# A hybrid encoder layer: the scan's decay rows and time steps computed another way, and its first part put in a program block of its own

## The chip, the cores and the metric

The kernel runs on one core of one Trainium2 chip. The metric is the device time of one execution in microseconds (us). Three runs of the kernel before took 1328.16, 1330.67 and 1332.90 us, so the median is 1330.67 us. One more execution was profiled; all rows below are from it.

## The reference

One encoder layer over 512 tokens of width 1024, in fp32. What is computed, cut to its core:

```
h = rms_norm(x);  z, xBC, dt_f, dt_b, q, k, v, gates = split(h @ w_in)
xs, B, C = split(silu(conv5(xBC)))                # depthwise, over tokens
dt = softplus(dt_raw + bias);  a = -exp(a_log)    # 32 heads, two directions
A = cumsum(dt * a) inside chunks of 128 tokens    # forward and backward
y = sum_s (C_l . B_s) exp(A_l - A_s) dt_s x_s     # inside a chunk, s <= l (or >=)
  + exp(A_l) C_l . state                          # what the chunks before carry in
y = group_rms_norm((y_f + y_b + D * xs) * silu(z));  ssd = y @ w_br_ssd
attn = windowed GQA with rotary q/k and a sink, @ w_br_attn
x += (sigmoid(g1) * ssd + sigmoid(g2) * attn) @ w_out
x += cross_attention(rms_norm(x), rms_norm(mem));  x += swiglu_ffn(rms_norm(x))
out = rms_norm(x)
```

The change touches the lines from `dt` to the inside of `y` (the "scan").

## The kernel before

All activations are held transposed: 128 partitions of channels by 512 tokens, eight such slabs for the width of 1024. A projection is one weight granule of 128 by 1024 (512 KB) that SyncE (SP) loads (line 120, tile `raw`); ScalarE (ACT) rounds it to a high part `whi` (line 128), VectorE (DVE) or, for some, GpSimd (POOL) makes the low part `wlo` (line 129), and TensorE (PE) runs 24 matmuls of 512 columns into one PSUM bank `mm` (lines 138 to 140: high by high, high by low, low by high). `raw` has two buffers, `whi` and `wlo` three, and a load is written two granules ahead of its use.

The stages in order: keys and values of the memory, the norm of x, the scan branch in four groups of eight heads, attention, the merge, cross-attention, the FFN. The scan branch ends near 562 us of the span.

`dt_step` (line 338) comes once, ahead of the groups. It has the 64 rows of raw time steps (32 heads, two directions) as 64 partitions by 512 tokens in `x1`, and makes softplus there on DVE with a polynomial (lines 348 to 358: fourteen alternating multiplications and additions, lines 354 and 355, a reciprocal, line 349, and others). Three results are then turned to token rows by twelve PE transposes (line 368). From them come the cumulative decays: `fm` (line 380), written to DRAM as `adr` (line 383), and `nb`, `wt`, `dec`, which stay on the chip.

For each head, `head` (line 522) takes two rows of `adr`, each spread by DMA over all 128 partitions (tile `rt`, line 516, three buffers). ACT makes their exponentials for the later scaling into `ear` (line 528, one tile for a pair of heads, two buffers); POOL masks both triangles (line 530); for direction 0 ACT makes exp(row + nb) in four instructions of 128 columns (line 536), for direction 1 DVE adds `nb` in four (line 538) and ACT makes one exponential of 512 columns (line 539). `both` adds the two on POOL (line 545), `times` multiplies by `cb` on DVE (line 550, tile `mt`). `inner` (PE, line 560) uses `mt`, `arrive` (line 572) the carried states, `gather` (lines 580 to 585) scales the second by `ear` and adds, its last addition on POOL (line 585). `weigh` (POOL, line 492, tile `xw`) and `carry` (PE, line 500) build the states. `conv` (lines 408 to 414) is the convolution after a projection; `x_turn` (line 467) transposes a finished `xs` on PE, one or two projections later.

Work is written as a list of `steps`, scan steps woven between projections, and the framework turns the list into one instruction stream for each engine. An engine takes its stream strictly in order: an instruction that waits holds all behind it on its engine; SP's loads are such a stream too.

Of the kernel before, what the change touches and what calls it, by code (L numbers as in the profile page):

```python
# [37 lines left out]
V_DTB, V_AL, V_DSK, V_SNK = 200, 201, 202, 218  # L38
V_N = 234
# [23 lines left out]
RAWB, WB = 2, 3  # L63

# [8 lines left out]
def bidir_hybrid_layer(ctx: ExitStack, tc: tile.TileContext, io, dbg=None):  # L73
# [17 lines left out]
    adr = dram.tile([64, S], F32, tag="adr", name="adr")  # L91

# [245 lines left out]
    def dt_step(w):  # L338
        acc = proj(w, st["hh"], st["hl"])
        v, e, den, s2, pl = (x1[0:64, i] for i in range(5))  # L340

        def t256(i, o):
            return x1[:, i, 256 * o:256 * o + 256].rearrange("p (c e) -> p c e", c=NCH)

        nc.scalar.activation(v, acc[0:64], AF.Identity, bias=vec[0:64, V_DTB:V_DTB + 1])
        nc.scalar.activation(e, v, AF.Abs)
# [5 lines left out]
        nc.vector.tensor_scalar(pl, s2, 2.0 / 17.0, 2.0 / 15.0, op0=ALU.mult, op1=ALU.add)  # L352
        for n in (13, 11, 9, 7, 5, 3, 1):
            nc.vector.tensor_tensor(pl, pl, s2, op=ALU.mult)
            nc.vector.tensor_scalar(pl, pl, 2.0 / n, None, op0=ALU.add)
        nc.vector.tensor_tensor(pl, pl, e, op=ALU.mult)
        dt, dta, ld = den, s2, e
        nc.vector.scalar_tensor_tensor(dt, v, 0.0, pl, op0=ALU.max, op1=ALU.add)
        an = st["sp"].tile([64, 1], F32, tag="an", name="an")
        nc.scalar.activation(an, vec[0:64, V_AL:V_AL + 1], AF.Exp)  # L360
        nc.vector.tensor_scalar(dta, dt, an, -1.0, op0=ALU.mult, op1=ALU.mult)
        nc.vector.tensor_scalar(ld, dt, 1e-37, None, op0=ALU.max)
        nc.scalar.activation(ld, ld, AF.Ln)

        def tok(src, o):
            b = bank("sb")
            for c in range(NCH):
                nc.tensor.transpose(b[:, c * 64:(c + 1) * 64], src[:, c * P:(c + 1) * P], ident[0:64, 0:64])
            nc.scalar.copy(o, b[:, 0:256].rearrange("p (c e) -> p c e", c=NCH))
            return o  # L370

        dat = tok(dta, t256(5, 0))
        dtt = tok(dt, t256(5, 1))
        ldt = tok(ld, t256(7, 1))
# [3 lines left out]
        for d in range(2):  # L378
            for c in range(NCH):
                nc.tensor.matmul(fm[32 * d:32 * d + 32, c * P:(c + 1) * P], dat[:, c, 32 * d:32 * d + 32],  # L380
                                 tri[d], start=True, stop=True)
        nc.scalar.copy(x1[0:64, 6], fm[0:64])
        nc.sync.dma_start(adr, x1[0:64, 6])
        tm = bank("sb")
        tv = tm[:, 0:256].rearrange("p (c e) -> p c e", c=NCH)
        for d in range(2):
            nc.tensor.matmul(tv[:, :, 32 * d:32 * d + 32], tri[d], dat[:, :, 32 * d:32 * d + 32],
                             start=True, stop=True)
        tot = bank("sb")
        ov = tot[:, 0:256].rearrange("p (c e) -> p c e", c=NCH)  # L390
        nc.tensor.matmul(ov, ones, dat, start=True, stop=True)
        acm = t256(4, 0)
        nc.scalar.copy(acm, tv)
        nc.scalar.activation(dec, ov, AF.Exp)
        nc.vector.tensor_tensor(nb, ldt, acm, op=ALU.subtract)
        nc.vector.tensor_tensor(wt, ov, acm, op=ALU.subtract)
        nc.scalar.activation(wt, wt, AF.Exp)
        nc.vector.tensor_tensor(wt, wt, dtt, op=ALU.mult)
# [87 lines left out]
    def group_scan(g):  # L486
# [355 lines left out]
    win = io["w_in"]  # L842
    opens("mo")
# [320 lines left out]
def layout(inputs):  # L1164
# [22 lines left out]
    vecs[0:32, V_AL] = a["a_log_fwd"][0]  # L1187
    vecs[32:64, V_AL] = a["a_log_bwd"][0]
# [34 lines left out]
```

## Time and profile before

| what | value |
|---|---|
| median of three runs | 1330.67 us |
| the profiled execution | 1331.93 us |
| its span (first to last instruction) | 1330.2 us |
| PE busy | 1259.6 us, 95% of the span |
| DVE, ACT, POOL busy | 811.2, 579.1, 316.4 us |
| mean granted clock of PE | 0.984 of full speed |

"Busy" adds up the time in which an engine has an instruction at work. On PE matmuls overlap, so it says that PE has work, not that it runs at its best rate. The views below list, besides busy time, what ended each idle stretch of an engine ("waits"), and the clock that PE was granted, as a share of 2.4 GHz.

### The profile page before, as it was taken

Reading aid. Unit: us, or ns where it says so; the run is one execution under the profiler, and the core shown is the slowest. Engines: PE = TensorE matmul, PEld = TensorE weight load, DVE = VectorE, ACT = ScalarE, POOL = GpSimd, SP = SyncE. Lnnn points to the kernel's source line nnn. Section 1 sums busy time; section 2 is a strip of 40 time slices with the busy share of each in tenths; the row PEclk is TensorE's granted clock in tenths of the full one; section 3 lists DMA queues with packets and bytes.
Section 4 is the critical chain, followed back from the end, with each engine's and each line's share of the span. In section 5 each row is a group of like instructions: output and inputs, shape, how many; then the busy total and the mean of one; then the engine's idle time right before and its main releaser. Section 6 shows DMA issues by size and latency. Waiting matters only on the chain.

```text
span 1330.2 us, 16362 instructions
## 1 busy us (share of the span) xinstructions
PE 1259.6 (95%) x6084; PEld 1016.9 (76%) x6084; DVE 811.2 (61%) x1359; ACT 579.1 (44%) x1001; POOL 316.4 (24%) x259
## 2 busy tenths in 40 slices
PE   6879998998999899999999999999999999999996
PEld 5667777786777687887667888888888888888886
DVE  5896788789678876678875334665443334442323
ACT  6437366266346434167865223444332223332220
POOL 3344263244354452321000002001121111110001
PEclk9999999999999899999999999999999999999998
DMA  6425344243233332321103333411232332223331
GB/s 241 141 97 151 123 151 127 60 131 116 82 103 111 95 96 90 113 88 64 49 33 111 98 98 106 143 64 52 92 96 97 102 102 95 96 91 103 88 99 64
DMA packets 45440, 134.95 MB, mean 101 GB/s; under 512 B 5104, under 2 KB 8560, under 8 KB 45360
## 3 DMA queue, kind: packets, MB, share of 16 engines
q1 hardware_dynamic: 43072, 129.77, 30.8%
q10 hardware_dynamic: 1584, 2.03, 0.5%
q0 software_dynamic: 704, 2.10, 0.4%
q8 instruction: 48, 0.79, 0.2%
q14 instruction: 32, 0.26, 0.1%
HBM read 129.55 MB, written 4.33 MB: 101 GB/s over the span
## 4 chain that ended last, share of the span: by engine, by line
PE 62%; DVE 12%; issue 10%; POOL 7%; ACT 5%; DMA 2%; SPq 0%; DVEq 0%; POOLq 0%; ACTq 0%
PE mm L138 18%; PE mm L139 18%; PE mm L140 18%; DVE rt L538 2%; DVE cvu L411 2%; DVE wlo L129 2%; POOL vv L585 1%; PE sb L815 1%; POOL mt L545 1%; ACT whi L128 1%; PE sb L802 1%; DMA rt<-adr 1%; POOL rsw L714 1%; POOL rt L530 1%; PE sb L988 1%
## 5 line engine op out<-in xcount | busy, mean ns | idle before, releaser
L128 ACT CAST whi<-raw 128x1024 fp32r<-128x1024 f32 (+2 forms) x192 | 198.9, 1037 | 451.9 <-PE mm L139 388.2
L138 PE MATMUL mm<-hh,whi 128*128 128x512 f32 x968 | 384.9, 398 | 6.9 <-DVE cvu L411 5.4
L139 PE MATMUL mm<-hl,whi 128*128 128x512 f32 x968 | 380.4, 393 | 1.8 <-DVE hl L310 1.8
L140 PE MATMUL mm<-hh,wlo 128*128 128x512 f32 x968 | 380.6, 393 | 1.1 <-DVE wlo L129 1.0
L129 DVE TENSOR_TENSOR wlo<-raw,whi 128x1024 fp32r<-128x1024 f32 (+2 forms) x193 | 242.4, 1257 | 128.4 <-ACT whi L128 122.4
L138 PEld LDWEIGHTS mm<-hh,whi 128*128 128x128 f32 x968 | 183.8, 190 | 46.3 <-issue 8.2
L140 PEld LDWEIGHTS mm<-hh,wlo 128*128 128x128 f32 x968 | 183.4, 189 | 41.3 <-DVE wlo L129 2.9
L139 PEld LDWEIGHTS mm<-hl,whi 128*128 128x128 f32 x968 | 183.6, 190 | 39.3 <-DVE hl L310 3.0
L185 POOL TENSOR_TENSOR sq_acc<-sq_acc,sq 128x512 f32<-128x512 f32 x14 | 24.8, 1771 | 264.4 <-ACT sq L184 264.4
L1041 POOL TENSOR_TENSOR fa<-fa,row 128x512 f32<-128x512 f32 x22 | 39.1, 1776 | 192.4 <-ACT fa L1040 192.4
L411 DVE SCALAR_TENSOR_TENSOR cvu<-mm,hcw,cvu 128x510 f32<-128x510 f32 (+1 forms) x96 | 70.9, 739 | 4.3 <-ACT cvu L408 3.9
L138 PE MATMUL mm<-vh,whi 128*128 128x512 f32 (+1 forms) x192 | 72.5, 378 | 0.0
L138 PE MATMUL mm<-fh,whi 128*128 128x512 f32 (+1 forms) x198 | 72.4, 366 | 0.0
L139 PE MATMUL mm<-fl,whi 128*128 128x512 f32 (+1 forms) x198 | 72.4, 365 | 0.0
L140 PE MATMUL mm<-fh,wlo 128*128 128x512 f32 (+1 forms) x198 | 72.4, 365 | 0.0
L140 PE MATMUL mm<-vh,wlo 128*128 128x512 f32 (+1 forms) x192 | 70.0, 364 | 0.0
L139 PE MATMUL mm<-vl,whi 128*128 128x512 f32 (+1 forms) x192 | 69.5, 362 | 0.0
L538 DVE TENSOR_SCALAR rt<-rt,nb 128x128 f32<-128x128 f32 x128 | 52.4, 465 | 21.3 <-POOL rt L530 19.6
L545 POOL TENSOR_TENSOR mt<-rt 128x512 f32<-128x512 f32 x32 | 47.7, 1493 | 72.1 <-ACT rt L539 34.1
L1043 DVE TENSOR_TENSOR ft<-fa,mm 128x512 f32<-128x512 f32 x22 | 15.1, 688 | 73.2 <-PE mm L140 71.0
L528 ACT ACTIVATE ear<-rt 64x1024 f32<-64x1024 f32 x32 | 33.9, 1059 | 56.6 <-POOL vv L585 51.9
L139 PE MATMUL mm<-ol,whi 128*128 128x512 f32 x128 | 50.0, 391 | 0.0
(234 smaller groups left out, 2061.4 us busy)
## 6 DMA issues: line engine op xcount, KB each, us to landing
raw<-in_w_in SPq DMA_DIRECT2D x69, 512.0 KB, 3.5
raw<-in_w_fi SPq DMA_DIRECT2D x44, 512.0 KB, 3.5
rt<-adr SPq DMA_DIRECT2D x64, 256.0 KB, 4.4
raw<-in_w_bs SPq DMA_DIRECT2D x16, 512.0 KB, 3.4
raw<-in_w_fo SPq DMA_DIRECT2D x16, 512.0 KB, 3.5
raw<-in_w_xk SPq DMA_DIRECT2D x8, 512.0 KB, 3.8
raw<-in_w_ba SPq DMA_DIRECT2D x8, 512.0 KB, 3.5
raw<-in_w_mo SPq DMA_DIRECT2D x8, 512.0 KB, 3.5
```

The lines of the kernel that those rows point to most:

```text
L128: nc.scalar.copy(hi[:, t], raw[:, t])
L129: (nc.gpsimd if i in LO_POOL else nc.vector).tensor_tensor(lo[:, t], raw[:, t], hi[:, t].bitcast(F32), op=ALU.subtract)
L138: nc.tensor.matmul(acc, wh, xh[:, k0 + k], start=first and k == 0, stop=False)
L139: nc.tensor.matmul(acc, wh, xl[:, k0 + k], start=False, stop=False)
L140: nc.tensor.matmul(acc, wl, xh[:, k0 + k], start=False, stop=last and k == nk - 1)
L185: eng.tensor_tensor(acc, acc, sq, op=ALU.add)
L411: nc.vector.scalar_tensor_tensor(u[:, b], acc[:, a], w5[j], u[:, b], op0=ALU.mult, op1=ALU.add)
L528: nc.scalar.activation(st["ear", h // 2][own], rt[own], AF.Exp)
L538: nc.vector.tensor_scalar(r, r, st["nb"][:, c, e0:e0 + 1], None, op0=ALU.add)
L545: nc.gpsimd.tensor_tensor(mt, st["rt", g, h][:, 0], st["rt", g, h][:, 1], op=ALU.add)
L1041: nc.gpsimd.tensor_tensor(a, a, st["row2"], op=ALU.mult)
L1043: nc.vector.tensor_tensor(t, a, st["fp", 2 * j + 1], op=ALU.mult)
```

## The change

Five things are done, all ahead of the end of the scan branch.

1. `dt_step` turns the raw time steps to token rows first (four transposes, line 352 of the new kernel) and does softplus on 128 partitions by 256, with each multiplication and addition of the polynomial in one instruction (line 364). `a_log` arrives as a row for every partition, so `vecs` is 297 columns wide, not 234.
2. The exponentials of the decay rows are made once, on 64 partitions (`erows`), and written to DRAM as `edr`; `ear` is filled from there by DMA, two loads a pair of heads (`earows`), in place of ACT's line 528.
3. Both directions of `rt` come in one DMA of 512 KB, not two of 256 KB.
4. For direction 1, ACT adds `nb` inside its exponential, in four instructions as for direction 0; DVE's line 538 and ACT's line 539 are gone.
5. The first part of the program, to the end of the scan branch, is a block in which the streams are ordered event by event along a timeline (`schedule_with_timeline_sim=True`); the rest is ordered as before. Each engine gets a branch into the block and one out of it. Behind the block the streams of PE, ACT, POOL and SP are the same as before, instruction for instruction (buffer numbers apart); DVE's differ at its first four places.

```diff
+EL = (2, 4)
...
     def dt_step(w):
         acc = proj(w, st["hh"], st["hl"])
-        v, e, den, s2, pl = (x1[0:64, i] for i in range(5))
-
-        def t256(i, o):
-            return x1[:, i, 256 * o:256 * o + 256].rearrange("p (c e) -> p c e", c=NCH)
-
-        nc.scalar.activation(v, acc[0:64], AF.Identity, bias=vec[0:64, V_DTB:V_DTB + 1])
-        nc.scalar.activation(e, v, AF.Abs)
+
+        def slot(i):
+            return x1[:, i // 2, 256 * (i % 2):256 * (i % 2) + 256].rearrange("p (c e) -> p c e", c=NCH)
+
+        v, e, den, s2, pl, dta, ld, acm = (slot(i) for i in range(8))
+        raw, rows, erows = (x1[0:64, i] for i in (5, 6, 7))
+        nc.scalar.activation(raw, acc[0:64], AF.Identity, bias=vec[0:64, V_DTB:V_DTB + 1])
+        tp = bank("sb")
+        tpv = tp[:, 0:256].rearrange("p (c e) -> p c e", c=NCH)
+        for c in range(NCH):
+            nc.tensor.transpose(tpv[:, c], raw[:, c * P:(c + 1) * P], ident[0:64, 0:64])
+        an = st["sp"].tile([P, 64], F32, tag="an", name="an")
+        nc.scalar.activation(an, vec[:, V_AL:V_AL + 64], AF.Exp)
+        nc.scalar.activation(e, tpv, AF.Abs)
+        nc.vector.tensor_copy(v, tpv)
         nc.scalar.activation(e, e, AF.Exp, scale=-1.0)
         nc.vector.tensor_scalar(den, e, 2.0, None, op0=ALU.add)
         nc.vector.reciprocal(den, den)
         nc.vector.tensor_tensor(e, e, den, op=ALU.mult)
         nc.vector.tensor_tensor(s2, e, e, op=ALU.mult)
-        nc.vector.tensor_scalar(pl, s2, 2.0 / 17.0, 2.0 / 15.0, op0=ALU.mult, op1=ALU.add)
-        for n in (13, 11, 9, 7, 5, 3, 1):
-            nc.vector.tensor_tensor(pl, pl, s2, op=ALU.mult)
-            nc.vector.tensor_scalar(pl, pl, 2.0 / n, None, op0=ALU.add)
-        nc.vector.tensor_tensor(pl, pl, e, op=ALU.mult)
-        dt, dta, ld = den, s2, e
+        nc.vector.tensor_scalar(pl, s2, 2.0 / 17.0, None, op0=ALU.mult)
+        for n in (15, 13, 11, 9, 7, 5, 3):
+            nc.vector.scalar_tensor_tensor(pl, pl, 2.0 / n, s2, op0=ALU.add, op1=ALU.mult)
+        nc.vector.scalar_tensor_tensor(pl, pl, 2.0, e, op0=ALU.add, op1=ALU.mult)
+        dt = den
         nc.vector.scalar_tensor_tensor(dt, v, 0.0, pl, op0=ALU.max, op1=ALU.add)
-        an = st["sp"].tile([64, 1], F32, tag="an", name="an")
-        nc.scalar.activation(an, vec[0:64, V_AL:V_AL + 1], AF.Exp)
-        nc.vector.tensor_scalar(dta, dt, an, -1.0, op0=ALU.mult, op1=ALU.mult)
+        anb = an.rearrange("p (o e) -> p o e", o=1).broadcast_to([P, NCH, 64])
+        nc.vector.scalar_tensor_tensor(dta, dt, -1.0, anb, op0=ALU.mult, op1=ALU.mult)
         nc.vector.tensor_scalar(ld, dt, 1e-37, None, op0=ALU.max)
-        nc.scalar.activation(ld, ld, AF.Ln)
-
-        def tok(src, o):
-            b = bank("sb")
-            for c in range(NCH):
-                nc.tensor.transpose(b[:, c * 64:(c + 1) * 64], src[:, c * P:(c + 1) * P], ident[0:64, 0:64])
-            nc.scalar.copy(o, b[:, 0:256].rearrange("p (c e) -> p c e", c=NCH))
-            return o
-
-        dat = tok(dta, t256(5, 0))
-        dtt = tok(dt, t256(5, 1))
-        ldt = tok(ld, t256(7, 1))
         nb, wt, dec = (st[n] for n in ("nb", "wt", "dec"))
         tri = [st["tri"][:, d] for d in range(2)]
...
-                nc.tensor.matmul(fm[32 * d:32 * d + 32, c * P:(c + 1) * P], dat[:, c, 32 * d:32 * d + 32],
+                nc.tensor.matmul(fm[32 * d:32 * d + 32, c * P:(c + 1) * P], dta[:, c, 32 * d:32 * d + 32],
                                  tri[d], start=True, stop=True)
...
+        nc.vector.tensor_copy(rows, fm[0:64])
+        nc.sync.dma_start(adr, rows)
+        nc.scalar.activation(erows, rows, AF.Exp)
+        nc.sync.dma_start(edr, erows)
         nc.scalar.copy(acm, tv)
         nc.scalar.activation(dec, ov, AF.Exp)
-        nc.vector.tensor_tensor(nb, ldt, acm, op=ALU.subtract)
         nc.vector.tensor_tensor(wt, ov, acm, op=ALU.subtract)
         nc.scalar.activation(wt, wt, AF.Exp)
-        nc.vector.tensor_tensor(wt, wt, dtt, op=ALU.mult)
+        nc.vector.tensor_tensor(wt, wt, dt, op=ALU.mult)
+        nc.scalar.activation(ld, ld, AF.Ln)
+        nc.vector.tensor_tensor(nb, ld, acm, op=ALU.subtract)
...
         def rows(h):
             rt = st["sp"].tile([P, 2, S], F32, tag="rt", name="rt", bufs=RB)
             e0 = 8 * g + h
-            for d in range(2):
-                nc.sync.dma_start(rt[:, d], adr[32 * d + e0:32 * d + e0 + 1, :].broadcast_to([P, S]))
+            nc.sync.dma_start(rt, adr.rearrange("(d e) s -> e d s", d=2)[e0:e0 + 1].broadcast_to([P, 2, S]))
             st["rt", g, h] = rt
+
+
+        def earows(i):
+            def f():
+                st["ear", i] = ear = st["sp"].tile([P, 2, S], F32, tag="ear", name="ear", bufs=2)
+                for k in range(2):
+                    e0 = 8 * g + 2 * i + k
+                    nc.sync.dma_start(ear[64 * k:64 * k + 64], edr.rearrange("(d e) s -> e d s", d=2)[e0:e0 + 1]
+                                      .broadcast_to([64, 2, S]))
+            return f
 
         def head(h):
             def f():
-                sp = st["sp"]
                 for n in (range(RB) if h == 0 else [h + RB - 1] if h + RB - 1 < HPG else []):
                     rows(n)
                 rt = st["rt", g, h]
-                if h % 2 == 0:
-                    st["ear", h // 2] = sp.tile([P, 2, S], F32, tag="ear", name="ear", bufs=2)
-                own = slice(64 * (h % 2), 64 * (h % 2) + 64)
-                nc.scalar.activation(st["ear", h // 2][own], rt[own], AF.Exp)
                 for d in range(2):
                     nc.gpsimd.affine_select(
                         out=rt[:, d].rearrange("p (c l) -> p c l", c=NCH),
                         in_=rt[:, d].rearrange("p (c l) -> p c l", c=NCH), pattern=[[0, NCH], [1 - 2 * d, P]],
                         base=0, channel_multiplier=2 * d - 1, compare_op=ALU.is_ge, fill=neg)
-                for c in range(NCH):
-                    r, e0 = rt[:, 0, c * P:(c + 1) * P], 8 * g + h
-                    nc.scalar.activation(r, r, AF.Exp, bias=st["nb"][:, c, e0:e0 + 1])
-                    r, e0 = rt[:, 1, c * P:(c + 1) * P], e0 + 32
-                    nc.vector.tensor_scalar(r, r, st["nb"][:, c, e0:e0 + 1], None, op0=ALU.add)
-                nc.scalar.activation(rt[:, 1], rt[:, 1], AF.Exp)
+                for d in range(2):
+                    for c in range(NCH):
+                        r, e0 = rt[:, d, c * P:(c + 1) * P], 32 * d + 8 * g + h
+                        nc.scalar.activation(r, r, AF.Exp, bias=st["nb"][:, c, e0:e0 + 1])
             return f
...
-                order.append(ga[(t - LAG3 - GLAG) // 2])
+                i = (t - LAG3 - GLAG) // 2
+                order += [ga[i]] + el[i + 2:i + 3]
+            if t in EL:
+                order.append(el[EL.index(t)])
...
+    cutat = len(steps)
     opens("mo")
     opens("at")
     add(at_open)
...
     ready, taken = [], 0
+    blk = ExitStack()
+    blk.enter_context(tc.block(schedule_with_timeline_sim=True))
     for i, (fn, gr) in enumerate(steps):
+        if i == cutat:
+            blk.close()
         ahead = LOOK if i >= lead else (i - lead + 4) // 2
         while len(ready) < min(len(specs), taken + len(gr) + ahead):
```

Three places show what is moved. The first is DVE at the end of the first group's scan, before: the four instructions of line 411 and line 414 finish a convolution into `xs`, which PE then transposes.

```order
L550 TENSOR_TENSOR mt_2004<-mt_2004,cb_1302 128x512
L411 SCALAR_TENSOR_TENSOR cvu_1770<-mm_1745,hcw_410,cvu_1770 128x510
L538 TENSOR_SCALAR rt_1989<-rt_1989,nb_170 128x128
L411 SCALAR_TENSOR_TENSOR cvu_1770<-mm_1745,hcw_410,cvu_1770 128x511
L129 TENSOR_TENSOR wlo_1794<-raw_1791,whi_1793 128x1024
L411 SCALAR_TENSOR_TENSOR cvu_1770<-mm_1745,hcw_410,cvu_1770 128x511
L538 TENSOR_SCALAR rt_1989<-rt_1989,nb_170 128x128
L411 SCALAR_TENSOR_TENSOR cvu_1770<-mm_1745,hcw_410,cvu_1770 128x510
L538 TENSOR_SCALAR rt_1989<-rt_1989,nb_170 128x128 x2
L550 TENSOR_TENSOR mt_2056<-mt_2056,cb_1302 128x512
L129 TENSOR_TENSOR wlo_1828<-raw_1825,whi_1827 128x1024
L414 SCALAR_TENSOR_TENSOR xs_1744<-cvt_1776,cvu_1770 128x512
```

The same place now, where the convolution has lines 409 and 412:

```order
L131 TENSOR_TENSOR wlo_1763<-raw_1760,whi_1762 128x1024
L409 SCALAR_TENSOR_TENSOR cvu_1739<-mm_1714,hcw_412,cvu_1739 128x510
L409 SCALAR_TENSOR_TENSOR cvu_1739<-mm_1714,hcw_412,cvu_1739 128x511 x2
L409 SCALAR_TENSOR_TENSOR cvu_1739<-mm_1714,hcw_412,cvu_1739 128x510
L131 TENSOR_TENSOR wlo_1797<-raw_1794,whi_1796 128x1024
L479 SCALAR_TENSOR_TENSOR zs_1791<-zs_1791,mm_1766 128x512
L412 SCALAR_TENSOR_TENSOR xs_1713<-cvt_1745,cvu_1739 128x512
L131 TENSOR_TENSOR wlo_1841<-raw_1838,whi_1840 128x1024
```

Four additions to `rt`, the multiplications into `mt` and one `wlo` no longer stand between the parts of the convolution.

The second is PE there. Before, the transpose of this `xs` stands between two projections (`mm_1831`, `mm_1876`):

```order
L139 MATMUL mm_1831<-hl_169,whi_1740 128x512
L140 MATMUL mm_1831<-hh_168,wlo_1741 128x512
L467 MATMUL sb_1859<-cst_77,xs_1744 128x128 x4
L138 MATMUL mm_1876<-hh_168,whi_1793 128x512
L139 MATMUL mm_1876<-hl_169,whi_1793 128x512
```

Now it stands inside the second of them, behind eleven of its 24 matmuls, the last three of which are shown:

```order
L142 MATMUL mm_1845<-hh_170,wlo_1763 128x512
L140 MATMUL mm_1845<-hh_170,whi_1762 128x512
L141 MATMUL mm_1845<-hl_171,whi_1762 128x512
L465 MATMUL sb_1828<-cst_78,xs_1713 128x128 x4
L142 MATMUL mm_1845<-hh_170,wlo_1763 128x512
L140 MATMUL mm_1845<-hh_170,whi_1762 128x512
```

The transpose has moved eleven matmuls back in PE's stream.

The third is SP at the start of the first group's scan. Before, where `adr` is written and the first rows are fetched:

```order
L120 DMA raw_848<-in_w_in 128x1024
L120 DMA raw_895<-in_w_in 128x1024
L383 DMA adr_74<-x1_69 64x512
L120 DMA raw_929<-in_w_xk 128x1024
L516 DMA rt_1084<-adr_74 128x512 x2
L516 DMA rt_1087<-adr_74 128x512 x2
L516 DMA rt_1090<-adr_74 128x512 x2
L120 DMA raw_975<-in_w_in 128x1024
```

Now:

```order
L122 DMA raw_833<-in_w_in 128x1024
L387 DMA adr_74<-x1_69 64x512
L389 DMA edr_75<-x1_69 64x512
L513 DMA rt_1069<-adr_74 128x2x512
L513 DMA rt_1071<-adr_74 128x2x512
L513 DMA rt_1073<-adr_74 128x2x512
L522 DMA ear_1162<-edr_75 64x2x512 x2
L522 DMA ear_1278<-edr_75 64x2x512 x2
L122 DMA raw_880<-in_w_in 128x1024
L122 DMA raw_914<-in_w_xk 128x1024
```

The write of `adr` stands one weight load earlier, `edr` and four loads of `ear` are new, and both weights that follow (`raw_880`, `raw_914`) stand behind all of them.

## Rows read from the trace of the kernel before

**Rows 1.** the page: span, busy time of each engine with its share

```profile
span 1330.2 us, 16362 instructions
...
PE 1259.6 (95%) x6084; PEld 1016.9 (76%) x6084; DVE 811.2 (61%) x1359; ACT 579.1 (44%) x1001; POOL 316.4 (24%) x259
```

**Rows 2.** busy time by stretch, us: PE, PEld, DVE, ACT, POOL; clock, DMA share

```profile
300.00:340.00 40.00, 33.38 (x158) 26.89 (x158) 33.43 (x54) 24.35 (x44) 15.52 (x15) 0.91 0.42 128
...
1000.00:1100.00 100.00, 100.00 (x443) 82.80 (x442) 41.82 (x48) 30.01 (x38) 16.05 (x9) 1.00 0.29 95
```

**Rows 3.** the waits of PE up to 562 us: total us, times, longest

```profile
PE sb L467 <- DVE xs L414: 19.9, 6, 5.7
...
PE mm L138 <- DVE cvu L411: 5.4, 3, 2.2
PE sb L500 <- POOL xw L492: 5.0, 6, 1.7
PE sb L368 <- DVE x L361: 4.2, 1, 4.2
PE sa L560 <- DVE mt L550: 2.9, 1, 2.9
```

**Rows 4.** PE in order of time, three of those: start, us, [idle before <- releaser]

```profile
193.80 0.65 PE L467 MATMUL sb<-cst,xs 128*128 128x128 f32 x4 [2.76 <-DVE xs L414]
...
225.06 0.63 PE L467 MATMUL sb<-cst,xs 128*128 128x128 f32 x4 [4.16 <-DVE xs L414]
...
333.11 1.09 PE L467 MATMUL sb<-cst,xs 128*128 128x128 f32 x4 [5.70 <-DVE xs L414]
```

**Rows 5.** busy time by stretch, the 20 us before one of those waits ends

```profile
205.00:225.00 20.00, 15.90 (x72) 12.80 (x71) 20.00 (x34) 13.87 (x26) 8.76 (x8) 1.00 0.52 157
```

**Rows 6.** the same with line 538 alone; the sum is over six stretches

```profile
205.00:225.00 20.00, 5.73 (x12) 1.00 0.52 157
...
sum 120.00, DVE 25.23; mean DVE 4.20
```

**Rows 7.** busy time in the eight half-clock stretches of the first 562 us

```profile
195.00:198.40 3.40, 3.40 (x23) 3.07 (x19) 1.70 (x2) 1.47 (x2) 2.24 (x2) 0.51 0.33 98
...
331.60:338.40 6.80, 5.29 (x15) 4.35 (x16) 4.99 (x7) 4.35 (x7) 2.11 (x2) 0.50 0.64 193
444.20:451.00 6.80, 5.92 (x20) 5.26 (x21) 5.42 (x9) 2.48 (x4) 3.06 (x3) 0.50 0.65 187
...
sum 34.00, PE 31.61 PEld 26.06 DVE 25.65 ACT 14.06 POOL 13.26; mean PE 3.95 PEld 3.26 DVE 3.21 ACT 1.76 POOL 1.66
```

**Rows 8.** groups by line, 0 to 566 us: busy us, mean ns, idle before

```profile
L538 DVE TENSOR_SCALAR rt<-rt,nb 128x128 f32<-128x128 f32 x128 | 52.4, 465 | 21.3 <-POOL rt L530 19.6 <-DMA raw<-in_w_in 1.7
...
L536 ACT ACTIVATE rt<-rt,nb 128x128 f32<-128x128 f32 x128 | 41.0, 391 | 0.5 <-POOL rt L530 0.2
...
L528 ACT ACTIVATE ear<-rt 64x1024 f32<-64x1024 f32 x32 | 33.9, 1059 | 56.6 <-POOL vv L585 51.9 <-DMA rt<-adr 4.2
...
L539 ACT ACTIVATE rt<-rt 128x512 f32<-128x512 f32 x32 | 19.9, 627 | 12.8 <-DVE rt L538 12.8
...
L398 DVE TENSOR_TENSOR wt<-wt,x 128x256 f32<-128x256 f32 x1 | 0.4, 420 | 0.0
```

**Rows 9.** time-step instructions on DVE: ns min/median/max, first and last start us

```profile
L354 DVE TENSOR_TENSOR x<-x x7: 670/672/2876, 67.7 to 86.2; 64x512 f32<-64x512 f32 x7
...
L349 DVE RECIPROCAL x<-x x1: 3333/3333/3333, 58.7 to 58.7; 64x512 f32<-64x512 f32 x1
```

**Rows 10.** the same by stretch: us, DVE busy (instructions), clock, DMA share

```profile
57.00:96.00 39.00, 26.82 (x23) 1.00 0.34 113
```

**Rows 11.** the waits of all engines, 0 to 566 us: total us, times, longest

```profile
ACT ear L528 <- POOL vv L585: 51.9, 14, 8.2
...
PEld mm L138 <- issue: 9.2, 16, 2.6
```

**Rows 12.** what the DMA queue on SP waited for, 0 to 566 us

```profile
SPq L120 <- DVE wlo L129: 305.7, 67, 15.5
```

More of the change, by code (lines that the diff above doesn't have):

```diff
@@ L37 @@
 V_CW, V_CB, V_SSD = 40, 160, 184
-V_DTB, V_AL, V_DSK, V_SNK = 200, 201, 202, 218
-V_N = 234
+V_DTB, V_DSK, V_SNK, V_AL = 200, 201, 217, 233
+V_N = 297
 G_DT, G_K, G_V, G_Q, G_GA, G_SSD, G_GS, G_N = 0, 1, 3, 5, 13, 21, 61, 69
@@ L91, in bidir_hybrid_layer @@
     adr = dram.tile([64, S], F32, tag="adr", name="adr")
+    edr = dram.tile([64, S], F32, tag="edr", name="edr")
     def bank(tag):
@@ L379, in dt_step @@
             for c in range(NCH):
-                nc.tensor.matmul(fm[32 * d:32 * d + 32, c * P:(c + 1) * P], dat[:, c, 32 * d:32 * d + 32],
+                nc.tensor.matmul(fm[32 * d:32 * d + 32, c * P:(c + 1) * P], dta[:, c, 32 * d:32 * d + 32],
                                  tri[d], start=True, stop=True)
-        nc.scalar.copy(x1[0:64, 6], fm[0:64])
-        nc.sync.dma_start(adr, x1[0:64, 6])
         tm = bank("sb")
@@ L386, in dt_step @@
         for d in range(2):
-            nc.tensor.matmul(tv[:, :, 32 * d:32 * d + 32], tri[d], dat[:, :, 32 * d:32 * d + 32],
+            nc.tensor.matmul(tv[:, :, 32 * d:32 * d + 32], tri[d], dta[:, :, 32 * d:32 * d + 32],
                              start=True, stop=True)
@@ L390, in dt_step @@
         ov = tot[:, 0:256].rearrange("p (c e) -> p c e", c=NCH)
-        nc.tensor.matmul(ov, ones, dat, start=True, stop=True)
-        acm = t256(4, 0)
+        nc.tensor.matmul(ov, ones, dta, start=True, stop=True)
+        nc.vector.tensor_copy(rows, fm[0:64])
+        nc.sync.dma_start(adr, rows)
+        nc.scalar.activation(erows, rows, AF.Exp)
+        nc.sync.dma_start(edr, erows)
         nc.scalar.copy(acm, tv)
         nc.scalar.activation(dec, ov, AF.Exp)
-        nc.vector.tensor_tensor(nb, ldt, acm, op=ALU.subtract)
         nc.vector.tensor_tensor(wt, ov, acm, op=ALU.subtract)
         nc.scalar.activation(wt, wt, AF.Exp)
-        nc.vector.tensor_tensor(wt, wt, dtt, op=ALU.mult)
+        nc.vector.tensor_tensor(wt, wt, dt, op=ALU.mult)
+        nc.scalar.activation(ld, ld, AF.Ln)
+        nc.vector.tensor_tensor(nb, ld, acm, op=ALU.subtract)
         dump("dt", dt)
@@ L605, in group_scan @@
         hd, bo, ti = ([w(h) for h in range(HPG)] for w in (head, both, times))
-        nn, ar, ga, gs = ([w(i) for i in range(4)] for w in (inner, arrive, gather, gate))
+        nn, ar, ga, gs, el = ([w(i) for i in range(4)] for w in (inner, arrive, gather, gate, earows))
         order = []
@@ L1186, in layout @@
     vecs[32:64, V_DTB] = a["dt_bias_bwd"][0]
-    vecs[0:32, V_AL] = a["a_log_fwd"][0]
-    vecs[32:64, V_AL] = a["a_log_bwd"][0]
+    vecs[:, V_AL:V_AL + 32] = a["a_log_fwd"][0][None]
+    vecs[:, V_AL + 32:V_AL + 64] = a["a_log_bwd"][0][None]
     vecs[:, V_DSK:V_DSK + 16] = _cols(np.repeat(a["d_skip"][0], 64))
```

## The prediction, made before the result was known

> **What bounds the kernel now.** The page is read first. PE is busy for 95% of the span, the next engine, DVE, for 61% [rows 1]. So PE sets the time, and the question is what PE loses. Second come the busy times by stretch. In the FFN, from 1000 to 1100 us, PE runs 443 matmuls of 512 columns in 100 us without a gap: 0.226 us each, its best rate, and DVE needs 42 of the 100 us. In the scan branch, from 300 to 340 us, PE is busy for 33.4 of 40 us at a mean clock of 0.91, and DVE for 33.4 as well [rows 2]. What can be won lies ahead of 562 us. Third come PE's own waits there. The largest kind by far is the transpose of a finished convolution (line 467) that waits for DVE's `xs`: 19.9 us in six places. Then come projections that wait for DVE to read a bank out (5.4), carries that wait for POOL's `xw` (5.0), the transposes in `dt_step` (4.2) and `inner` (2.9) [rows 3]. The order in time shows that the six are not noise: PE stands still for 2.8, 4.2 and 5.7 us with nothing else it may do [rows 4]. In the 20 us that end with the wait at 225 us DVE is busy for all 20 [rows 5], so PE waits there for a DVE that is behind. Fourth, the clock. Eight stretches ahead of 562 us, 34.0 us together, ran at 1.2 instead of 2.4 GHz [rows 7]. One begins at 195 us, right after the wait that ended at 193.8; one at 331.6, inside the wait that ends at 333.1. In them PE was busy for 31.6 us. Work at half rate costs half its time, so about 15.8 us were lost.
>
> **The change part by part.**
>
> Term A, the six transposes. Line 538 goes from DVE: 128 instructions, 52.4 us [rows 8]. In the six stretches of 20 us that end with the six waits it takes 25.2 us, more than the 19.9 us that PE waits; ahead of 225 us it is 5.7 us against a wait of 4.2 [rows 4, 6]. The order shows besides that the transpose at the end of the first group stands eleven matmuls later, worth 11 x 0.226 = 2.5 us, and that no `rt` work stands inside that convolution any more. Bounds: 0 (DVE fills the room with other work that is in front) and 19.9. I take 18, since relief exceeds the wait in sum and DVE, at 33.4 of 40 us in such a stretch, gives up 52.4 us over some 440 us of scan, near 5 in 40.
>
> ACT takes it over. For each head it had 1059 (ear) + 4 x 391 + 627 = 3250 ns; it will have 8 x 391 = 3128 ns [rows 8]. That is 0.1 us less a head, so nothing on ACT gets later. In such a stretch it is busy for 24.4 of 40 us [rows 2]. Cost: none. One load of `rt` in place of two carries the same bytes, and `vecs` is 32 KB larger: 0 for both, beside weight loads of 512 KB that PE does not wait for now.
>
> Term B, `dt_step`. On DVE its 23 instructions take 26.8 us between 57 and 96 us [rows 10], the reciprocal 3.3 of them [rows 9]. The new chain has twelve two-input instructions, a copy and three with a scalar on 128 x 256, each like the 0.42 us of line 398, and a reciprocal on half as many elements (half of 3.3): 16 x 0.42 + 1.7 = 8.4 us [rows 8, 9]. What hangs on DVE there is 4.2 us at the transposes and 5.4 us at the banks [rows 3]. Twelve transposes become four, which I don't count. Bounds 2 and 9.6; I take 7, nearer the upper end, for the chain is a third of what it was.
>
> Line 354 has a median of 672 ns, but one of its seven took 2876 [rows 9]; POOL makes `wlo` in that stretch. The Trainium skill (GPSIMD Engine Reference, Key points) says that GpSimd shares its SBUF interfaces with VectorE and contends with DVE instructions that have two SBUF inputs. That speaks against the new chain, whose steps nearly all have two: by the rule a few of them would take 2.2 us more, as that one did; with three such the chain is 15 us, term B 5 and not 7, and the sum 30 and not 32. The trace agrees as far as line 354 goes.
>
> Term C, the carries. Five us of waiting for POOL's `xw` come at the start of the groups, where POOL is late with masks because ACT's `ear` held it up: ACT stood 51.9 us waiting for POOL to free an `ear` [rows 11]. That hold is gone from ACT. POOL's own work stays. Bounds 0 and 5.0; I take 3.
>
> Term D, the clock. Of the eight half-clock stretches five follow waits of terms A and B (96, 195, 225.8, 331.6 and 444.2 us). Each of the three short ones costs 3.4/2 = 1.7, the two long ones 5.29/2 and 5.92/2 by their busy time [rows 7]: 3 x 1.7 + 2.6 + 3.0 = 10.7. Bounds 0 and 15.8; I take 9, since A and B are not taken in full either.
>
> Term E, what is new. First, in-order waits: the event order puts `inner` one instruction at a time between matmuls, where a late `mt` holds PE at once. The nearest row is the single wait of 2.9 us at `inner` [rows 3]; sixteen pairs of heads could each meet one, so the bounds are 0 and 46. I take 4, nearest to the row as it is. Second, SP: `ear` adds 32 loads of 256 KB, and ahead of the first group two weights stand behind seven loads. SP waits 305.7 us in 67 places for `wlo` to free a buffer [rows 12], 4.6 us a load, which is the slack that hides this; if it were gone, one load's wait would reach PE. I take 0 here, and the rival below prices it. Third, the border of the blocks. No row shows it: bounds 0 and 2.6, the longest that PE's weight loads stood for no reason shown [rows 11]; I take 1. The Trainium skill (Advanced Engine Details and Errata, Control Flow Timing) gives about 51 ns for a branch; by that the term would be 0.05 us, which no row here shows. Fourth, the start: all four loads of x now stand ahead of the third weight, which delays that weight and brings the norm forward; I take 0.
>
> Behind the block nothing moves on PE, so the 768 us from 562 to the end of the span stay.
>
> Sum: 18 + 7 + 3 + 9 - 4 - 1 = 32 us less. From the profiled execution's own 1331.9 us that gives 1299.9. The median of the runs is 1.3 us below the profiled one, so the forecast for a median is 1299 us.
>
> **The rivals.**
>
> *All waits go.* If the terms come at their upper bounds and the 2.9 us at `inner` go as well: 19.9 + 9.6 + 5.0 + 2.9 + 15.8 - 1 = 52 us, so 1279 us for a median. For it: with line 538 gone DVE has 12 of 40 us free, and in the FFN, where it has more, PE loses nothing [rows 2]. Against: one of the half-clock stretches (at 21 us) lies ahead of all that the change touches.
>
> *Half.* The DVE relief comes, but order positions set ahead of what the engines do cost much of it back: say 16 places x 1 us at `inner`, and the clock falls after them (5 us). 32 - 12 - 5 = 15, so 1316 us. For it: durations on DVE vary fourfold from one instance to the next [rows 9], and no fixed order can know that.
>
> *No change.* PE's wait moves to POOL, which still masks and adds for every `mt`: 1331 us. Against: POOL is busy for 24% of the span [rows 1], and for 8.8 of 20 us at the wait of 225 us [rows 5].
>
> *Slower: SP holds the weights.* The wait for POOL to free an `ear` moves from ACT to SP, where weight loads stand behind it: 14 places, 51.9 us, longest 8.2 [rows 11]. It decides from the point where a held `ear` outlasts the 4.6 us of slack of a load. With a mean of 3.7 us most are hidden; if all came through to PE, 51.9 - 32 = 20 us more than now, so 1351 us.
>
> **How the numbers follow.** The forecast case (1284 to 1314; its terms at their nearer bounds) 0.50; all waits go, or most of it (below 1284) 0.14; half (1314 to 1326) 0.16; no change 0.07; slower 0.13. About 0.3%, 4 us, is what a measurement of this kernel can tell from no change. Faster then has 0.80, within it 0.07, slower 0.13. The range that holds 8 in 10 runs from 1276, with 0.07 below it, to 1332, with 0.13 above it.
>
> **What would show it.** Right for A: in the new profile the waits of `x_turn` (line 465 there) sum to under 3 us, DVE in the first 540 us is some 70 us less busy. For B: the waits of PE at lines 352 and 376 sum to under 3 us. For D: at most four half-clock stretches ahead of the end of the scan branch. For E: a line of PE waits at `inner`, line 560, of some 4 us; SP's waits for `ear`, line 522, under 4.6 us each. The scan branch should end near 530 us, and the rest should take the same time. The prediction is wrong if PE's waits stay near 48 us under other names, if PE waits for `whi` or `wlo` because loads are late, or if the part behind the block gets longer.

## The result and the profile after

The changed kernel takes 1306.29 us (median of four runs, 1304.91 to 1307.29), the kernel before 1330.82 beside it: a ratio of 0.9816, 95% interval 0.980 to 0.983. That is 24.5 us less; 32 were forecast. Its profiled execution takes 1304.91 us. Why it is faster turned out to be another matter than the prediction says.

Busy times from the page of the changed kernel, as the second line of [rows 1]; its span is 1303.1 us:

```profile
PE 1251.0 (96%) x6076; PEld 1011.3 (78%) x6076; DVE 772.1 (59%) x1226; ACT 564.3 (43%) x1062; POOL 313.2 (24%) x259
```

Busy time up to the end of the scan branch, which now comes near 536 us, and behind it (columns as in [rows 2]):

```profile
0.00:536.00 536.00, 497.54 (x2530) 399.00 (x2530) 390.16 (x511) 260.54 (x524) 226.55 (x202) 0.99 0.47 140
...
536.00:1303.10 767.10, 753.50 (x3548) 612.33 (x3546) 381.95 (x715) 303.74 (x538) 86.63 (x57) 0.99 0.28 89
```

The whole gain lies ahead of 536 us: the rest takes 767.1 us, and took 768.2. What PE waits for up to 545 us, as [rows 3]:

```profile
PE mm L140 <- DVE cvu L409: 13.7, 3, 6.4
...
PE sb L465 <- DVE xs L412: 2.4, 2, 1.7
PE sb L498 <- POOL xw L490: 2.3, 2, 2.0
...
PE sa L560 <- DVE mt L550: 1.0, 2, 0.8
```

The 19.9 us at `x_turn` are 2.4, the 4.2 in `dt_step` are gone, the carries have 2.3 for 5.0. But the waits for a bank that a convolution has to read out (`cvu`) have grown from 5.4 to 13.7, in three places, and the longest two are these:

```profile
74.93 0.77 PE L140 MATMUL mm<-hh,whi 128*128 128x512 f32 x1 [4.66 <-DVE cvu L409]
...
119.56 0.77 PE L140 MATMUL mm<-hh,whi 128*128 128x512 f32 x1 [6.40 <-DVE cvu L409]
```

The half-clock stretches ahead of the end of the scan, as [rows 7]; there were eight, of 34.0 us:

```profile
74.90:78.30 3.40, 3.37 (x8) 2.73 (x9) 3.40 (x7) 1.49 (x2) 1.84 (x1) 0.50 0.22 89
115.80:122.60 6.80, 3.04 (x7) 2.48 (x8) 4.99 (x6) 5.15 (x15) 2.47 (x5) 0.50 0.70 167
371.80:375.20 3.40, 3.40 (x11) 2.61 (x10) 2.42 (x4) 3.40 (x12) 3.40 (x4) 0.51 0.00 0
```

### The profile page after: what moved, and what is told of

It reads as the page before. It is cut to its first block, busy times and chain, and to the rows that moved or that the text cites. A ratio compares the mean times of both kernels' runs of the same rounds, so it can differ in the third digit from the quotient of the medians.

```text
span 1303.1 us, 16244 instructions
## 1 busy us (share of the span) xinstructions
PE 1251.0 (96%) x6076; PEld 1011.3 (78%) x6076; DVE 772.1 (59%) x1226; ACT 564.3 (43%) x1062; POOL 313.2 (24%) x259
## 4 chain that ended last, share of the span: by engine, by line
PE 59%; issue 6%; DVE 2%; ACT 1%; POOL 1%; DMA 0%; DVEq 0%; POOLq 0%; ACTq 0%
PE mm L140 18%; PE mm L142 18%; PE mm L141 18%; PE sb L818 1%; PE sb L805 1%; POOL rsw L717 1%; PE sb L992 1%; PE sa L961 1%; PE sa L777 1%; PE sa L779 0%; PE sb L172 0%; PE sb L572 0%; ACT whi L130 0%; PE sb L155 0%; ACT rsw L716 0%
## 5 line engine op out<-in xcount | busy, mean ns | idle before, releaser
L131 DVE TENSOR_TENSOR wlo<-raw,whi 128x1024 fp32r<-128x1024 f32 (+2 forms) x193 | 238.2, 1235 | 145.0 <-ACT whi L130 135.2
L539 ACT ACTIVATE rt<-rt,nb 128x128 f32<-128x128 f32 x256 | 78.8, 389 | 67.4 <-POOL rt L532 67.3
L532 POOL TENSOR_SCALAR_AFFINE_SELECT rt<-rt 128x512 f32<-128x512 f32 x64 | 47.6, 766 | 67.7 <-DMA rt<-adr 67.5
L142 PE MATMUL mm<-oh,wlo 128*128 128x512 f32 x128 | 50.0, 391 | 0.0
```

The source lines that it names most:

```text
L131: (nc.gpsimd if i in LO_POOL else nc.vector).tensor_tensor(lo[:, t], raw[:, t], hi[:, t].bitcast(F32), op=ALU.subtract)
L142: nc.tensor.matmul(acc, wl, xh[:, k0 + k], start=False, stop=last and k == nk - 1)
L532: nc.gpsimd.affine_select(out=rt[:, d].rearrange("p (c l) -> p c l", c=NCH), in_=rt[:, d].rearrange("p (c l) -> p c l", c=NCH), pattern=[[ ...
```

## The experiments

Theory 1 is the prediction's: line 538's 52 us off DVE end the waits at `x_turn`. Theory 2: the event order ends them, and the relief matters little. Times are medians, ratios against the kernel before, which took 1330.8 to 1332.8 us beside them.

**1. The parts, one by one.** Without the block (`e1_no_block`):

```diff
-    blk = ExitStack()
-    blk.enter_context(tc.block(schedule_with_timeline_sim=True))
...
-        if i == cutat:
-            blk.close()
```

> The changed kernel without the two blocks: new decays, new dt_step, ear and rt loads stay, the order is the one of the kernel before. Theory 1 (VectorE's relief makes the gain, the order little): the x_turn transposes still wait under 4 us in all, the half-clock stretches ahead of the end of the scan stay at four or fewer, and the time is 1306 to 1312 us. Theory 2 (the event order makes the gain): x_turn waits come back to over 10 us and the time is 1322 us or more.

1318.39 us, 0.990 (0.988 to 0.992). The kernel before with those lines and nothing else (`e2_block_only`):

> The kernel before with nothing but the first block put around the program to the end of the scan branch. Theory 1: VectorE still carries line 538's 52 us, so PE still waits some 15 us or more at x_turn; 1322 to 1333 us. Theory 2: 1304 to 1312 us, with x_turn under 5 us.

1308.65 us, 0.983 (0.981 to 0.985). And with the new decays alone, old `dt_step` and no block (`e6_decays_only`):

> The kernel before with the new decays alone (128 additions off VectorE, ear and rt by single loads), old dt_step, no block. Theory 1 as predicted (line 538's relief ends the x_turn waits): x_turn waits under 4 us and 1308 to 1316 us. Theory 2 (those waits are a matter of VectorE's order, not of its load): x_turn waits stay at 12 us or more and the time is 1322 to 1332 us.

1324.26 us, 0.995 (0.993 to 0.996). PE's waits at `x_turn` in the three, in that order:

```profile
PE sb L465 <- DVE xs L412: 20.3, 5, 8.0
```

```profile
PE sb L467 <- DVE xs L414: 0.8, 2, 0.4
```

```profile
PE sb L472 <- DVE xs L419: 18.0, 5, 8.9
```

Theory 1 falls for this wait. With line 538 gone but the old order the wait is as long as ever, 20.3 and 18.0 us; with line 538 in place and the event order it is gone. The times say the same less sharply: those of `e2_block_only` and `e6_decays_only` lie in theory 2's ranges, that of `e1_no_block` between the two theories. Without the block the other four parts still give 13.7 us (1332.1 to 1318.4), so the order is worth 23.5 us alone and 12.1 on top of them. Nor is DVE less busy when the wait goes. From 200 to 400 us with the block alone DVE is busy for 179 of 200 us, 24 us more than before (155.8), and PE loses less than 3:

```profile
200.00:400.00 200.00, 197.39 (x1015) 157.03 (x1014) 179.46 (x272) 110.64 (x191) 91.32 (x84) 1.00 0.40 115
```

What the order changes is shown by the last convolution of the scan. First the kernel before, in order of time: ACT starts to read the projection out, DVE finishes `xs`, PE transposes.

```profile
436.64 0.77 ACT L408 ACTIVATE cvu<-mm,hcw 128x512 f32<-128x512 f32 x1
...
444.25 0.68 DVE L414 SCALAR_TENSOR_TENSOR xs<-cvt,cvu 128x512 f32<-128x512 f32 x1
...
445.08 1.09 PE L467 MATMUL sb<-cst,xs 128*128 128x128 f32 x4 [4.22 <-DVE xs L414]
```

The same with the block alone:

```profile
419.18 0.77 ACT L408 ACTIVATE cvu<-mm,hcw 128x512 f32<-128x512 f32 x1
...
426.92 0.69 DVE L414 SCALAR_TENSOR_TENSOR xs<-cvt,cvu 128x512 f32<-128x512 f32 x1
...
428.31 0.60 PE L467 MATMUL sb<-cst,xs 128*128 128x128 f32 x4
```

The convolution takes 7.6 us in one and 7.7 in the other. But before, PE starts 17 matmuls between that readout and its transposes, 17 x 0.226 = 3.8 us of work, and then stands for 4.2; with the block it starts 41, 9.1 us of work (419.18 to 428.31), and does not stand. Counted over all 16 convolutions, the fewest matmuls in between are 14 before, 12 in `e1_no_block` and in `e6_decays_only`, and 41 with the block alone, though the mean time from the start of the readout to that of the instruction that finishes `xs` rose from 8.4 to 11.6 us there. With line 538 gone and the old order (`e6_decays_only`) this mean is 8.5 us: relief did not make DVE's convolutions come sooner. The wait was a matter of how far behind the order put PE's transposes, not of how fast DVE came.

**2. One part undone inside the block.** Line 538's additions back on DVE, `ear` still loaded (`e3_decays_dve`):

```diff
-                for d in range(2):
-                    for c in range(NCH):
-                        r, e0 = rt[:, d, c * P:(c + 1) * P], 32 * d + 8 * g + h
-                        nc.scalar.activation(r, r, AF.Exp, bias=st["nb"][:, c, e0:e0 + 1])
+                for c in range(NCH):
...
+                    nc.vector.tensor_scalar(r, r, st["nb"][:, c, e0:e0 + 1], None, op0=ALU.add)
+                nc.scalar.activation(rt[:, 1], rt[:, 1], AF.Exp)
```

> The changed kernel with one part undone: the second direction's 128 additions of nb go back to VectorE, with one ScalarE exponential of 512 columns per head behind them; ear stays loaded, dt_step and the blocks stay. Theory 1: terms A and D come back, x_turn waits 12 us or more, 1322 to 1331 us. Theory 2: the event order works round it, under 5 us more than the changed kernel, 1305 to 1311 us.

1328.2 us, 0.997 (0.996 to 0.998): the number of theory 1, for another reason. `x_turn` waits only 3.3 us here. The loss is in `cvu`, 7.8 us more than in the changed kernel, and in the clock that falls after such waits: 37.5 us of half-clock stretches ahead of the end of the scan, where the changed kernel has 13.6.

```profile
PE mm L140 <- DVE cvu L409: 21.5, 5, 9.1
```

The old `dt_step` instead (`e4_old_dt`):

> The changed kernel with the dt_step of before (64 partitions x 512 columns, 23 VectorE instructions, three rounds of transposes), plus the exponential and the store of edr that the loaded ear needs. Term B as forecast (7 us, with the clock of one stretch 9): 1311 to 1316 us, with PE waiting 3 us or more at the dt transposes. As the changed trace reads (the new chain's wait only moved into the mm banks, cvu waits 13.7 us where 9.6 stood): 1303 to 1309 us, and the cvu waits fall by 4 us or more.

1314.11 us, 0.988 (0.986 to 0.989). The new `dt_step` is worth 7.8 us. The wait at the transposes does not come back; PE waits at `inner` in its place, 9.7 us where it was 1.0, since all that hangs on the time steps is later: the last group of `dt_step`'s matmuls starts at 110.7 us, with the new one at 87.3. One sign of the other theory came too: the `cvu` waits fall from 13.7 to 8.8 us.

```profile
PE sa L567 <- DVE mt L557: 9.7, 7, 6.5
```

**3. Which half of the decays costs.** The block with the new `dt_step`, nothing else (`e5_block_and_dt`):

> The kernel before with the block and the new dt_step, and nothing else of the change: ear still comes from ScalarE, line 538's additions stay on VectorE, rt in two loads. If the parts add up (block alone 1308.65 us; old dt_step in place of the new one cost 1314.11 - 1306.29 = 7.8 us): 1299 to 1303 us. If the new dt_step is worth something only beside the new decays: 1306 to 1311 us.

1300.64 us, 0.976 (0.975 to 0.978): faster than the whole change. So inside the block the new decays cost 5.7 us, which they do beside the old `dt_step` as well (1314.11 - 1308.65 = 5.5). On top of it only the additions moved to ACT, `ear` still made by ACT and `rt` in two loads (`e9_add_on_act`):

```diff
-                    nc.vector.tensor_scalar(r, r, st["nb"][:, c, e0:e0 + 1], None, op0=ALU.add)
-                nc.scalar.activation(rt[:, 1], rt[:, 1], AF.Exp)
+                        nc.scalar.activation(r, r, AF.Exp, bias=st["nb"][:, c, e0:e0 + 1])
```

> The kernel of the run with block and dt_step alone (1300.64 us), with line 538's 128 additions moved to ScalarE as in the change, but ear still made by ScalarE and rt still in two loads. It tells which half of the new decays costs 5.6 us inside the block. If the loads of ear cost it (GpSimd 67.5 us behind rt in the changed kernel): 1296 to 1302 us, GpSimd's waits for rt under 15 us. If ScalarE's extra step costs it (128 x 391 - 32 x 627 = 30 us more of ScalarE, its copies whi and cvu later): 1304 to 1310 us.

1289.2 us, 0.968 (0.967 to 0.970), beyond both expectations. The additions on ACT are worth 11.4 us in the event order; `ear` by DMA and `rt` in one load, the rest of the step to the changed kernel, cost 17.1. With the additions on DVE the same loads cost more, 27.6 us (1300.64 to 1328.2), and beside the loads the additions on ACT are worth more, 21.9 (1328.2 to 1306.29). So the relief of DVE does pay, though not at `x_turn`. What POOL's masks wait for, first in the changed kernel, then in this one:

```profile
POOL rt L532 <- DMA rt<-adr: 67.5, 24, 5.6
```

```profile
POOL rt L524 <- ACT ear L522: 14.0, 11, 2.6
```

With the `ear` loads the masks wait for `rt` to land, 67.5 us in 24 places. Without them ACT reads `rt` first, for `ear`, and waits only 5.4 us for it to land; POOL waits 14.0 for ACT. It is not that `rt` comes much later: in both runs SP issues its load as soon as the buffer is free (0.2 us behind that in the mean in the changed kernel, 0.0 in this one), and the loads land after 5.5 and 4.5 us by the median. What differs is the place of the masks in POOL's stream. They stand 0.2 us behind the landing in the changed kernel, 19.1 us behind it here, in the mean of the 32 heads. So POOL waits at a mask while the additions into `mt` stand behind it. One such place in the changed kernel: the exponentials that the addition needs are done at 107.75 us and POOL is free at 108.93, but the mask of the next head comes first.

```profile
103.66 4.09 ACT L539 ACTIVATE rt<-rt,nb 128x128 f32<-128x128 f32 x13
...
106.39 2.54 POOL L545 TENSOR_TENSOR mt<-rt 128x512 f32<-128x512 f32 x2
113.59 1.23 POOL L532 TENSOR_SCALAR_AFFINE_SELECT rt<-rt 128x512 f32<-128x512 f32 x2 [4.65 <-DMA rt<-adr]
114.79 1.26 POOL L545 TENSOR_TENSOR mt<-rt 128x512 f32<-128x512 f32 x1
```

In this run, for the same two heads, the addition comes first:

```profile
113.46 1.43 POOL L537 TENSOR_TENSOR mt<-rt 128x512 f32<-128x512 f32 x1 [3.02 <-ACT rt L531]
114.85 1.67 POOL L524 TENSOR_SCALAR_AFFINE_SELECT rt<-rt 128x512 f32<-128x512 f32 x2
```

DVE shows what that place does to PE in the changed kernel. It takes its stream in order, and ahead of the wait of 6.40 us it stands for this `mt`, with three parts of the convolution behind it:

```profile
116.08 1.10 DVE L550 TENSOR_TENSOR mt<-mt,cb 128x512 f32<-128x512 f32 x1 [2.36 <-POOL mt L545]
117.10 2.31 DVE L409 SCALAR_TENSOR_TENSOR cvu<-mm,hcw,cvu 128x511 f32<-128x511 f32 x3
```

Whether the size of one load is part of it was tried with `rt` in two loads in the changed kernel (`e7_rt_two_loads`):

> The changed kernel with rt loaded as before, one load of 256 KB per direction in place of one of 512 KB. If the later landing of the 512 KB (5.5 us against 4.4 for 256 KB before) is what makes GpSimd's masks and with them mt late, so that VectorE stands at mt with a convolution behind it: GpSimd's waits for rt fall from 67.5 us to under 50, the waits of PE for cvu from 13.7 to under 9, 1299 to 1304 us. If not: 1305 to 1309 us.

1304.23 us, 0.978 (0.977 to 0.980). POOL's wait falls to 48.2 us, PE's for `cvu` to 8.8, but 5.2 us come up at a bank that `xw` holds. Both waits fell as the first theory had it; the intervals touch, so the 2 us are not certain. The loads of `ear` hold most of the 17 us: this run and `e9_add_on_act` differ in `ear` alone, by 15.0 us. That they cost it by the order on POOL is shown for the one wait above; for the whole it is likely by these rows and not shown, since no run keeps the loads and moves the masks.

**4. POOL beside DVE's new chain.** The other long wait, at 74.93 us, ends a stretch in which the chain of `dt_step` is slow. DVE, and then POOL, in the changed kernel:

```profile
62.19 0.41 DVE L360 TENSOR_TENSOR x<-x 128x256 f32<-128x256 f32 x1
...
63.19 2.54 DVE L361 TENSOR_TENSOR x<-x 128x256 f32<-128x256 f32 x1
65.76 2.37 DVE L362 TENSOR_SCALAR x<-x 128x256 f32<-128x256 f32 x1
...
70.57 0.74 DVE L409 SCALAR_TENSOR_TENSOR cvu<-mm,hcw,cvu 128x511 f32<-128x511 f32 x1
71.23 1.91 DVE L364 SCALAR_TENSOR_TENSOR x<-x 128x256 f32<-128x256 f32 x1
...
63.06 4.93 POOL L131 TENSOR_TENSOR wlo<-raw,whi 128x1024 fp32r<-128x1024 f32 x2 [3.31 <-ACT whi L130]
70.21 2.65 POOL L131 TENSOR_TENSOR wlo<-raw,whi 128x1024 fp32r<-128x1024 f32 x1 [2.22 <-PE mm L141]
```

Each long step of DVE starts inside a subtraction of POOL (2.4 to 2.6 us each) and ends 0.15 to 0.3 us after it. The nine subtractions back to DVE (`e8_lo_on_dve`):

```diff
-LO_POOL = range(10, 19)
+LO_POOL = range(0)
```

> The changed kernel with the nine wlo subtractions that GpSimd makes (loads 10 to 18) back on VectorE, nine of 1.2 us more for it. If VectorE's long steps in the dt chain (2.54, 2.37, 1.91, 1.75 and 1.61 us where the same forms take 0.41 or less) come from GpSimd working beside them, the longest of lines 358 to 370 but for the reciprocal is under 0.6 us, and the wait of 4.7 us at 75 us shrinks; the time is 1302 to 1308 us. If they have another cause, steps over 1.5 us stay and the time is 1306 to 1314 us.

The same three lines of that run (ns min/median/max, first and last start):

```profile
L364 DVE SCALAR_TENSOR_TENSOR x<-x x7: 413/416/426, 70.9 to 78.5; 128x256 f32<-128x256 f32 x7
...
L361 DVE TENSOR_TENSOR x<-x x1: 417/417/417, 67.0 to 67.0; 128x256 f32<-128x256 f32 x1
L362 DVE TENSOR_SCALAR x<-x x1: 283/283/283, 68.6 to 68.6; 128x256 f32<-128x256 f32 x1
```

So the cause is shown. The time is 1305.3 us, 0.980 (0.978 to 0.982), no sure gain: PE's excess (its time beyond that of its matmuls at their best rate) falls by 5 us between 40 and 80 us, and rises by 5 between 120 and 160, at `xw` and `mt`, which POOL makes there. The same edit where POOL is not late (`e10_lo_on_dve_best`, on the block with the new `dt_step`):

> The kernel with block and dt_step alone (1300.64 us), and the nine wlo subtractions of GpSimd on VectorE. If the contention of the two engines in the dt chain is what is left of the wait ahead of 100 us (it was worth 1.0 us of the time and 5 us of excess between 40 and 80 us beside the changed kernel): 1296 to 1300 us. If VectorE, 90% busy in the scan here, has no room for 11 us more: 1301 to 1306 us.

1291.6 us, 0.971 (0.969 to 0.972): 9.0 us less, more than either theory gave it. The two traces differ by 6.5 us, and PE's excess between 40 and 80 us by 4.7 of them; where the rest comes from is open.

**5. The border, and the best version.** The block and `dt_step`, with the whole program in one block (`e11_one_block`):

> The kernel with block and dt_step alone (1300.64 us), the whole program in one block ordered event by event, without a border at the end of the scan branch. If the border costs what the trace shows at it (some 2 us of stalls on PE between 560 and 600 us that the kernel before hasn't) and the event order does no harm behind it: 1294 to 1300 us. If the default order is the better one behind the scan, where PE is the bound: 1302 to 1325 us.

1324.46 us, 0.995 (0.993 to 0.996). The 2 us of stalls that were laid to the border are a wait for DVE's `mx` in the attention, which the kernel before has too (1.9 us at 608.6 us). The event order does harm behind the scan. The attention, from 640 to 712 us, has PE busy for 64 of 72 us, at a clock of 0.91:

```profile
640.00:712.00 72.00, 64.02 (x281) 37.86 (x281) 42.77 (x176) 44.99 (x132) 0.00 (x0) 0.91 0.05 13
```

With the border the same stage, from 590 to 700 us of the run with block and `dt_step`, loses 1 us of 110. Counted at the same projection matmul, the run with one block is 3.4 us late ahead of the attention, 22.5 behind it and 25.4 near the end of the trace:

```profile
590.00:700.00 110.00, 109.11 (x552) 76.42 (x549) 81.41 (x268) 80.44 (x206) 3.97 (x3) 1.00 0.19 63
```

All the winning edits together, additions and `ear` on ACT, `rt` in two loads, `wlo` on DVE (`e12_best`):

> Block, new dt_step, all decay additions on ScalarE, ear made by ScalarE, rt in two loads (1289.2 us), and the nine wlo subtractions of GpSimd on VectorE. If the parts add up (that last edit gave 1300.64 - 1291.6 = 9.0 us with the additions on VectorE): 1278 to 1283 us, and the excess of PE between 40 and 80 us falls from 8.6 to under 5 us. If what it gave there was room on VectorE that the additions on ScalarE have given already: 1286 to 1290 us.

1281.54 us, 0.963 (0.961 to 0.966): 24.8 us faster than the changed kernel. The parts add up: the last edit gives 7.7 us here, and PE's excess between 40 and 80 us falls from 8.6 to 2.3. Its busy times, in a span of 1278.5 us:

```profile
PE 1245.7 (97%) x6076; PEld 1011.1 (79%) x6076; DVE 771.7 (60%) x1235; ACT 595.1 (47%) x1093; POOL 293.9 (23%) x250
```

## Why the prediction was right in its number and wrong in its reason

The forecast's case (1284 to 1314) held, but by luck: the order was priced as a cost of 5 us and the loads at nothing, and they came to 23.5 us less and 17.1 more. By the runs the change is made of four pieces, each put on the one before: the event order -23.5 us (1332.1 to 1308.65), the new `dt_step` -8.0, the additions on ACT -11.4, the loads of `ear` and `rt` +17.1. Together that is -25.8; 1306.29 stands 24.5 under the 1330.8 measured beside it. The pieces are not fixed prices: put on last, the order gives 12.1; with the additions on DVE the loads cost 27.6; beside the loads the additions on ACT give 21.9. The steps, one by one:

- **Term A, the step that failed.** "Relief exceeds the wait in sum" put the 18 us down to line 538. The wait went as forecast (19.9 to 2.4), but the relief did not do it: 20.3 us stand without the block, 0.8 with the block alone. Taking line 538 off DVE is worth 11.4 to 21.9 us inside the block, but at other waits and through the clock. That DVE was busy for all 20 us ahead of one wait [rows 5] was read as DVE being too slow. It was busy with work that the order had put in front, and PE's transposes stood as few as 14 matmuls behind the start of a chain of 8 us. The prediction saw the one place where the transpose moved, eleven matmuls, and gave it 2.5 us; that was the mechanism.
- **Term E, the order** was priced as a cost alone, 4 us at `inner` and 1 at the border. `inner` waits 1.0 us, PE's longest wait between 460 us and the border is 1.4 us, as it is in the kernel before, and the order as a whole is the largest gain.
- **Term E, the loads: 0 forecast, 17 measured.** The rival "SP holds the weights" had nearly the size, 20 us, and not the way. SP does wait for `ear` longer than 4.6 us at times (line 522: 62.2 us in 13 places, longest 8.9), but PE's waits for `wlo` ahead of 545 us are 1.3 us in all, and the loads of `rt` are issued as their buffers come free. The term left out what the loads do to POOL's order (experiment 3).
- **Term B: 7 forecast, 7.8 and 8.0 measured**, though not by the way described. The chain's 17 instructions take 16.3 us of DVE where 8.4 were forecast. The waits it feeds did not shrink in the trace; what it brings is that everything behind the time steps comes earlier. The rule of the Trainium skill that spoke against it (GPSIMD Engine Reference, Key points) held, and more than three steps met it: its 15 us were nearer than the 8.4. Left alone, in `e8_lo_on_dve`, the 17 take 8.0 us, so the forecast priced a chain without POOL beside it. And the rule spoke against the old chain as much: six of its 23 steps were held, for 2.0 to 2.9 us, not the one that the prediction read in line 354. Line 355 has two of them:

```profile
L355 DVE TENSOR_SCALAR x<-x x7: 405/408/2582, 68.9 to 89.5; 64x512 f32<-64x512 f32 x7
```

- **Term C: 3 forecast**, 2.7 less wait at the carries, but not for the reason given. With ACT's hold gone and the old order (`e6_decays_only`) they wait 7.3 us; with the hold in place and the block alone, 3.0.
- **Term D: 9 forecast.** Half-clock time fell from 34.0 to 13.6 us, worth (31.6 - 9.8) / 2 = 10.9 by PE's busy time in it: the size forecast. It is not what the order's gain rests on: the block alone still has 27.3 us of it ahead of 560 us, with PE busy for 26.1, so 2.8 us of its 23.5 are the clock's.
- **The checks.** "DVE some 70 us less busy" was wrong, 430.0 to 390.2 us, 40 less. Line 538 and the chain gave 61; `mt` (line 550) took 14.5 back, 1151 ns each for 697: 21 of its 32 instructions start inside one of POOL's and take 1397 ns in the mean, the other 11 take 680.

## What to carry to other kernels

A wait for an engine that is busy is not yet a wait for an engine that is too slow: count the instructions that the waiting engine has between the producer's start and the wait, and compare their time with the producer's latency, before taking work off the producer. Price an order as a term that can gain, and try it alone. Of a bundle that wins, run the parts: here one of four cost 17 us or more that the other three hid.

## What was not expected of the hardware

GpSimd's subtraction of 128 x 1024 stops a VectorE instruction whole, not by a share: five of the chain's steps took 1.6 to 2.5 us and ended 0.15 to 0.3 us behind GpSimd's instruction, with 0.28 to 0.43 us for the same steps without it. It struck `tensor_scalar`, with one tensor input, too (2.37 and 1.75 us for 0.28). The Trainium skill (SBUF — State Buffer, SBUF: two separate sides) says so of instructions with two SBUF inputs or in a two-port mode, and that whichever starts first keeps the pair of ports for its whole instruction; these steps agree. The part of a convolution at 70.57 us, which has one of its inputs in PSUM, ran inside such a subtraction and took its usual 0.74 us.
